# Last product of the down-projection rearranged, and the second block's mixer inputs begun earlier, in a one-core decoder layer

## Chip, cores and metric

The kernel runs on one core of one Trainium2 chip. The metric is the device time of one execution in microseconds (us). The kernel before takes 2018.15 us, the median of three runs (2018.1 to 2020.99).

## What is computed

One decoder layer on 2048 tokens of width 1024, all in float32. Cut to what matters here:

```python
h = rmsnorm(x, norm_mix) * (1 + sc_m) + sh_m          # mixer inputs
bg, cg, hc, u, v = split(h @ w_in)                    # 512 columns each
y_a = short_conv_mixer(bg, cg, hc, conv_w)            # gated convolution, 3 taps
y_b = chunked_sgu_mixer(gelu(u), gelu(v), v_norm, w_s, b_s)
x = x + g_m * (concat(rmsnorm(y_a), rmsnorm(y_b)) @ w_out)
h = rmsnorm(x, norm_ffn) * (1 + sc_f) + sh_f
gate, up = split(h @ w_up)                            # d_ff = 2816
x = x + g_f * ((silu(gate) * up) @ w_down)
return rmsnorm(x, norm_final)
```

A scaling, shift and gate for each channel (sc, sh, g) come from the conditioning vector.

## The kernel before

Tokens lie along the free dimension, channels on the partitions. The 2048 tokens are four quarters of 512 (`Q`), two quarters to a block (`NB = 2`). Each matrix product of two float32 tiles is made of three passes of TensorE over split operands (`mm3`, L173 to L175): the high half of both, high times low, low times high. The high half is made by a cast on ScalarE (L151), the low half by a subtraction on VectorE (L152), so a weight tile is ready only when both engines have handled it. L173 and L174 need the high half of the weights, L175 the low half.

The program does for each block: convolution and mixer (`mixer`: the products v, then u for each of the two quarters), the output projection (`out_proj`: 16 tiles, eight for each quarter, names w_o and o), and the preparation of the feed-forward inputs. Then come the up-projection and the down-projection of both blocks. `prepare(1, hT)` makes the second block's mixer inputs: for each of its two quarters eight loads of x (xin), eight squares on ScalarE with seven additions on GpSimd (sx), a sum over channels on TensorE (ms_x, L146), a reciprocal root (ScalarE and four VectorE steps), eight scalings on GpSimd (L262), eight shifts on ScalarE (L263) and eight splits (h). It is a generator: the output projection of the first block calls it three steps at a time after every tile.

Both feed-forward products are of Strassen's kind: seven products in place of eight. The last of the down-projection's seven, P2, multiplies left tiles A12 (one for each of 11 pairs of d_ff tiles, `NPR = 11`) with right tiles B21 that hold both blocks. For each pair and block it has 12 products (four output tiles, three passes). The second block follows three pairs behind the first (`lag = 3`). A left tile is split once, and both blocks use it. After P2 each block gets its last update of x (L787), the squares of the first quarter (L852), their sum (ms_f), the root, the final scaling (L870) and the stores to the output (L873). The second quarter (index i = 1) is ready before P2, and its final normalising is asked for during P2's first pair, for both blocks one after the other. In the last call three of the eight tiles go to ScalarE and GpSimd (L867, L868).

Each engine works its own list in order. The order in the lists comes from a scheduler that runs when the program is built. It moves instructions between the points where the program text has them, and names such as `tc.issue_after` bind some to others. Loads and stores all stand in SP's list. Tiles come from pools with a fixed number of buffers: 6 for split weights (`wslot`), 14 panels (inputs and right tiles), 17 temporaries, 8 PSUM banks.

Of the kernel before, what the change touches and what calls it, by code (L numbers as in the profile page):

```python
# [20 lines left out]
Q = 512  # L21
NQ = S // Q
NB = 2
# [4 lines left out]
NPR = NJ // 2  # L28
# [14 lines left out]
def trunk_kernel(  # L43
# [17 lines left out]
    nc = tc.nc  # L61
# [10 lines left out]
    def ps_tile(name):  # L72
        return psum.tile([P, Q], F32, tag="ps", name=name)
# [20 lines left out]
    ones_d = const.tile([P, P], F32, name="ones_d")  # L94
# [41 lines left out]
    def rms_finish(ms, n, name):  # L136
        r = tmp(f"R_{name}")[:, :n]
        rsqrt_into(r, ms, n)
        return r

    def rms_rows(sums, ones, name, ms=None):

        n = sums[0].shape[-1]
        ms = (ms or ps_tile(f"ms_{name}"))[:, :n]
        for k, s in enumerate(sums):
            nc.tensor.matmul(ms, ones, s, start=k == 0, stop=k == len(sums) - 1)  # L146
        return rms_finish(ms, n, name)
# [6 lines left out]
    last = {}  # L154
# [119 lines left out]
    class Conv:  # L274
# [30 lines left out]
        def normalise(self, i):  # L305
            r = rms_rows([self.acc[i]], ones_c, f"a{self.b}_{i}")
            for ct in range(CT):
                nc.vector.tensor_mul(self.ya[i][:, ct, :], self.ya[i][:, ct, :], r)
# [445 lines left out]
    def down(last_pair):  # L754
# [5 lines left out]
        def left(prod, p):  # L760
            w = wslot(f"{LEFT[prod]}_d{p}")
            name = LEFT[prod]
            if name[0] == "A":
                src = wts[U_FF + 3 * (2 * p + int(name[2]) - 1) + 2][:, 512 * (int(name[1]) - 1):][:, :512]
            else:
                src = sd[p][:, ("S2", "S1", "S4", "S3").index(name), :]
            raw = tmp(f"raw_{name}_d{p}")
            last["load"] = nc.sync.dma_start(raw, src).ins
            split(w, raw)
            return w  # L770

        def right(prod, p):
            t = panel(f"{RIGHT[prod]}_d{p}", [P, 2, NB * Q])
            raw = rawslot(f"raw_{RIGHT[prod]}_d{p}")
            nc.sync.dma_start(raw, gd[p][RIGHT[prod]].rearrange("p b q -> p (b q)"))
            split(t, raw)
            return [t[:, :, b * Q:b * Q + Q] for b in range(NB)]

        def products(prod, p, b, w, t, first):
            for s in range(4):  # L780
                ssl = slice(s * P, s * P + P)
                mm3(ps[b, s], w[:, 0, ssl], w[:, 1, ssl], t[:, 0, :], t[:, 1, :],
                    first and p == 0, p == NPR - 1, not first)

        def update(b, s, hi, i):
            dt = s + 4 * hi
            nc.vector.scalar_tensor_tensor(  # L787
                out=x[b][dt][:, i], in0=ps[b, s], scalar=gcol(dt), in1=x[b][dt][:, i], op0=ALU.mult, op1=ALU.add
            )
# [6 lines left out]
        for prod in ORDER_DOWN[:-1]:  # L796
# [17 lines left out]
            for b in range(NB):  # L814
                for s in range(4):
                    update(b, s, *lands[prod])
        lag = 3
        ready = {}
        for n in range(NPR + lag):
            while len(ready) < min(n + 4, NPR):  # L820
                ready[len(ready)] = left("P2", len(ready)), right("P2", len(ready))
            for b in range(NB):
                p = n - b * lag
                if p == 0:
                    for s in range(4):
                        ps[b, s] = ps_tile(f"d_P2_{b}_{s}")
                if 0 <= p < NPR:
                    w, t = ready[p]
                    products("P2", p, b, w, t[b], True)
            if n == 0:  # L830
                for f in fs:
                    f.squares(1, range(4))
                for f in fs:
                    f.normalise(1)
            for b in range(NB):
                if n == NPR - 1 + b * lag:
                    for s in range(4):
                        update(b, s, 0, 0)
                        fs[b].square(0, s)
            if n == NPR:  # L840
                fs[0].normalise(0)
        fs[1].normalise(0, (2, 5, 7))

    class Finish:

# [12 lines left out]
                square_into(acc, self.x[dt][:, i], dt == dts[0], nc.gpsimd)  # L858
            self.sums.setdefault(i, []).append(acc)

        def normalise(self, i, shared=()):

            r = rms_rows(self.sums[i], ones_d, f"f{self.b}_{i}")
            for dt in range(KT):
                xi = self.x[dt][:, i]
                if dt in shared:
                    nc.scalar.mul(xi, xi, vcol(V_NFIN + dt))  # L867
                    nc.gpsimd.tensor_mul(xi, xi, r)  # L868
                else:
                    nc.vector.scalar_tensor_tensor(  # L870
                        out=xi, in0=xi, scalar=vcol(V_NFIN + dt), in1=r, op0=ALU.mult, op1=ALU.mult
                    )
                nc.sync.dma_start(outT[QB * self.b + i, :, dt, :], xi)  # L873
# [127 lines left out]
    def stepper(g, n=1):  # L1001
        return lambda: [next(g, None) for _ in range(n)]

    hT, conv, ws_sb = start()
    y, late = mixer(0, hT, conv, ws_sb, lambda: None)
    hT = []
    g = prepare(1, hT)
    out_proj(0, y, late, stepper(g, 3))
    for _ in g:
        pass  # L1010
    g = ffn_inputs(0)
# [86 lines left out]
```

## Time and profile before

| | |
|---|---|
| median of three runs | 2018.15 us |
| the profiled execution | 2017.61 us |
| its span, first to last instruction | 2015.9 us |
| granted clock of TensorE, mean | 0.99 of 2.4 GHz |
| TensorE busy | 1951.1 us, 97% |
| VectorE busy | 1153.5 us, 57% |
| ScalarE busy | 786.8 us, 39% |
| GpSimd busy | 633.7 us, 31% |
| time in which DMA queue q1 had packets, of 16 engines | 47.3% |

TensorE is busy nearly throughout, so a profile of shares tells little. What can be saved is where TensorE waits, where its clock is at the lower level, and what lies behind its last product. Times in the views count from the start of the span. In the rows PE is TensorE, DVE is VectorE, ACT is ScalarE, POOL is GpSimd, SPq is the queue that issues DMAs.

### The profile page before, as it was taken

Reading aid. Unit: us, or ns where it says so; the run is one execution under the profiler, and the core shown is the slowest. Engines: PE = TensorE matmul, PEld = TensorE weight load, DVE = VectorE, ACT = ScalarE, POOL = GpSimd, SP = SyncE. Lnnn points to the kernel's source line nnn. Section 1 sums busy time; section 2 is a strip of 40 time slices with the busy share of each in tenths; the row PEclk is TensorE's granted clock in tenths of the full one; section 3 lists DMA queues with packets and bytes.
Section 4 is the critical chain, followed back from the end, with each engine's and each line's share of the span. In section 5 each row is a group of like instructions: output and inputs, shape, how many; then the busy total and the mean of one; then the engine's idle time right before and its main releaser. Section 6 shows DMA issues by size and latency. Waiting matters only on the chain.

```text
span 2015.9 us, 23007 instructions
## 1 busy us (share of the span) xinstructions
PE 1951.1 (97%) x8424; PEld 1583.6 (79%) x8424; DVE 1153.5 (57%) x1595; ACT 786.8 (39%) x1314; POOL 633.7 (31%) x440
## 2 busy tenths in 40 slices
PE   5989998999999999999999999999999999999996
PEld 3778876788878877878888888888888888888874
DVE  7988667543277574454455856455455454454464
ACT  3442655322366453333333633333333332233221
POOL 3200025100420145554644475665563100011011
PEclk9999999999999999999999999999999999999998
DMA  8567354231546635334324644543546974243332
GB/s 277 188 207 263 106 197 152 89 120 58 178 149 227 209 101 177 124 110 163 140 105 145 237 162 145 180 156 138 180 160 217 351 268 137 94 150 114 133 120 84
DMA packets 136915, 328.21 MB, mean 163 GB/s; under 512 B 14305, under 2 KB 22497, under 8 KB 134498
## 3 DMA queue, kind: packets, MB, share of 16 engines
q1 hardware_dynamic: 136802, 326.74, 47.3%
q8 instruction: 66, 1.08, 0.2%
q14 instruction: 47, 0.39, 0.1%
HBM read 242.28 MB, written 84.41 MB: 162 GB/s over the span
## 4 chain that ended last, share of the span: by engine, by line
PE 61%; DVE 4%; DMA 3%; POOL 1%; issue 1%; ACT 1%; SPq 0%; DVEq 0%; POOLq 0%; ACTq 0%
PE gu_a L173 7%; PE gu_a L174 7%; PE gu_a L175 7%; PE d_P L173 7%; PE d_P L174 7%; PE d_P L175 7%; PE gu_d L173 4%; PE gu_d L174 4%; PE gu_d L175 4%; PE gu_e L175 2%; PE gu_e L174 2%; PE gu_e L173 2%; DMA raw_gu<-in_wts 1%; DMA raw_T<-hd_T 1%; DVE x L870 0%
## 5 line engine op out<-in xcount | busy, mean ns | idle before, releaser
L152 DVE TENSOR_TENSOR ws<-raw_gu,ws 128x512 fp32r<-128x512 f32 x176 | 193.9, 1139 | 151.1 <-ACT ws L151 139.7
L152 DVE TENSOR_TENSOR A<-raw_gu,A 128x512 fp32r<-128x512 f32 x132 | 103.7, 818 | 127.1 <-ACT A L151 126.9
L151 ACT CAST ws<-raw_gu 128x512 fp32r<-128x512 f32 x176 | 101.9, 617 | 139.8 <-PE gu_d L175 67.7
L615 POOL TENSOR_TENSOR raw_gu<-raw_gu 128x512 f32<-128x512 f32 x44 | 59.5, 1353 | 289.6 <-DMA raw_gu<-in_wts 257.5
L173 PE MATMUL gu_a<-T,ws 128*128 128x512 f32 x352 | 139.4, 396 | 0.0
L174 PE MATMUL gu_a<-T,ws 128*128 128x512 f32 x352 | 139.0, 395 | 0.0
L175 PE MATMUL gu_a<-T,ws 128*128 128x512 f32 x352 | 138.9, 395 | 0.0
L133 POOL TENSOR_TENSOR sf<-sf,sq 128x512 f32<-128x512 f32 x18 | 28.3, 1576 | 327.5 <-ACT sq L132 326.5
L175 PE MATMUL c<-h,w_c 128*128 128x512 f32 x320 | 125.3, 392 | 4.8 <-DVE w_c L152 4.8
L173 PE MATMUL c<-h,w_c 128*128 128x512 f32 x320 | 125.6, 393 | 0.7 <-DVE ya L301 0.6
L174 PE MATMUL c<-h,w_c 128*128 128x512 f32 x320 | 125.1, 391 | 0.5 <-DVE h L224 0.5
L173 PE MATMUL d_P<-T_d,S_d 128*128 128x512 f32 x264 | 102.7, 389 | 0.0
L174 PE MATMUL d_P<-T_d,S_d 128*128 128x512 f32 x264 | 102.7, 389 | 0.0
L175 PE MATMUL d_P<-T_d,S_d 128*128 128x512 f32 x264 | 102.7, 389 | 0.0
L481 POOL TENSOR_TENSOR b<-b,r 128x512 f32<-128x512 f32 x32 | 43.5, 1379 | 185.8 <-DVE ya L301 87.8
L133 POOL TENSOR_TENSOR sx<-sx,sq 128x512 f32<-128x512 f32 x14 | 21.0, 1498 | 232.8 <-ACT sq L132 231.9
L151 ACT CAST A<-raw_gu 128x512 fp32r<-128x512 f32 x132 | 78.7, 620 | 39.5 <-DMA raw_gu<-in_wts 23.9
L152 DVE TENSOR_TENSOR S_d<-raw_S_d,S_d 128x512 fp32r<-128x512 f32 x44 | 32.1, 733 | 93.9 <-ACT S_d L151 93.7
L174 PEld LDWEIGHTS gu_a<-T,ws 128*128 128x128 f32 x352 | 66.0, 187 | 16.3 <-issue 0.2
L173 PEld LDWEIGHTS gu_a<-T,ws 128*128 128x128 f32 x352 | 66.0, 187 | 16.3 <-issue 0.2
L175 PEld LDWEIGHTS gu_a<-T,ws 128*128 128x128 f32 x352 | 66.0, 187 | 16.2
L624 POOL TENSOR_TENSOR raw_gu<-raw_gu 128x512 f32<-128x512 f32 x44 | 63.8, 1468 | 41.4 <-DVE A L152 41.4
(256 smaller groups left out, 5528.5 us busy)
## 6 DMA issues: line engine op xcount, KB each, us to landing
raw_gu<-in_wts SPq DMA_DIRECT2D x88, 512.0 KB, 4.1
raw_T_d<-gd_T SPq DMA_DIRECT2D x44, 512.0 KB, 3.7
raw_B_d<-gd_B SPq DMA_DIRECT2D x33, 512.0 KB, 3.5
wm<-in_wmodT SPq DMA_DIRECT2D x32, 512.0 KB, 4.3
raw_o<-in_wts SPq DMA_DIRECT2D x32, 512.0 KB, 5.7
raw_c<-in_wts SPq DMA_DIRECT2D x28, 512.0 KB, 4.1
gd_B<-s SPq DMA_DIRECT2D x44, 256.0 KB, 7.0
gd_T<-s SPq DMA_DIRECT2D x44, 256.0 KB, 2.1
```

What stands on the lines that cost most here:

```text
L133: (add or nc.vector).tensor_add(acc, acc, sq)
L151: nc.scalar.copy(dst[:, 0, :], src)
L152: (sub or nc.vector).tensor_sub(dst[:, 1, :], src, dst[:, 0, :].bitcast(F32))
L173: nc.tensor.matmul(ps, l_hi, r_hi, start=start, stop=False, skip_group_check=onto)
L174: nc.tensor.matmul(ps, l_hi, r_lo, start=False, stop=False, skip_group_check=onto)
L175: nc.tensor.matmul(ps, l_lo, r_hi, start=False, stop=stop, skip_group_check=onto)
L481: nc.gpsimd.tensor_mul(t, t, rs[i])
L615: nc.gpsimd.tensor_add(a21, a21, a22)
L624: nc.gpsimd.tensor_sub(a12, a12, a11)
```

## The change

There are two parts.

In the program's end (`down`), the second block follows six pairs behind the first. Left tiles are loaded and split for each block by itself, three pairs ahead; right tiles three pairs ahead. The normalising of the second quarter stands after the third pair for the first block and after the fifth for the second block. The first block's last normalising (ScalarE multiplies, GpSimd scales, all eight tiles) stands after pair 6 of the second block. The second block's last three pairs are done output tile by output tile: nine products, then one sum matmul for the tile before (ms_last), the update and the square. The last scaling is all on VectorE.

In the mixer, `prepare` is called from the mixer of the first block after 14 steps without work, one step at a time, and in the output projection two steps at a time in place of three.

```diff
-        def products(prod, p, b, w, t, first):
-            for s in range(4):
+        def products(prod, p, b, w, t, first, ss=range(4)):
+            for s in ss:
...
-        lag = 3
-        ready = {}
+        lag = 6
+        rights, lefts = {}, {}
         for n in range(NPR + lag):
-            while len(ready) < min(n + 4, NPR):
-                ready[len(ready)] = left("P2", len(ready)), right("P2", len(ready))
+            while len(rights) < min(n + 3, NPR):
+                rights[len(rights)] = right("P2", len(rights))
             for b in range(NB):
                 p = n - b * lag
+                for k in range(5 if n == NPR + 1 else 3):
+                    if 0 <= p + k < NPR and (b, p + k) not in lefts:
+                        lefts[b, p + k] = left("P2", p + k)
...
-                if 0 <= p < NPR:
-                    w, t = ready[p]
-                    products("P2", p, b, w, t[b], True)
+                if 0 <= p < NPR - 3 * b:
+                    products("P2", p, b, lefts[b, p], rights[p][b], True)
             if n == 0:
                 for f in fs:
                     f.squares(1, range(4))
-                for f in fs:
-                    f.normalise(1)
...
-            if n == NPR:
-                fs[0].normalise(0)
-        fs[1].normalise(0, (2, 5, 7))
+            if n in (2, 4):
+                fs[n // 2 - 1].normalise(1)
+            if n == NPR - 1:
+                for s in range(4):
+                    update(0, s, 0, 0)
+                    fs[0].square(0, s)
+            if n == NPR + 1:
+                fs[0].normalise(0, spare=True)
+        for s in range(4):
+            for p in range(NPR - 3, NPR):
+                products("P2", p, 1, lefts[1, p], rights[p][1], True, [s])
+            if s == 0:
+                ms = ps_tile("ms_last")
+            nc.tensor.matmul(ms, ones_d, fs[1].sums[0][s], start=s == 0, stop=False)
+            update(1, s, 0, 0)
+            fs[1].square(0, s)
+        nc.tensor.matmul(ms, ones_d, fs[1].sums[0][4], start=False, stop=True)
+        fs[1].normalise(0, rms_finish(ms, Q, "last"))
...
-    y, late = mixer(0, hT, conv, ws_sb, lambda: None)
-    hT = []
-    g = prepare(1, hT)
-    out_proj(0, y, late, stepper(g, 3))
+    h0, hT = hT, []
+    def later():
+        for _ in range(14):
+            yield
+        yield from prepare(1, hT)
+    g = later()
+    y, late = mixer(0, h0, conv, ws_sb, stepper(g))
+    out_proj(0, y, late, stepper(g, 2))
```

How the lists of the engines stand. First SP, where the loads of the second block's first quarter (xin) are issued; raw_o are the weights of the output projection, x_0 the first block's residual, xd its copy in memory. Before:

```order
L158 DMA raw_o_0_1_2234<-in_wts 128x1024
L422 DMA x_0_1_2165<-in_xT 128x2x512 x2
L158 DMA raw_o_0_2_2311<-in_wts 128x1024
L158 DMA raw_o_0_3_2358<-in_wts 128x1024
L158 DMA raw_o_0_4_2415<-in_wts 128x1024
L158 DMA raw_o_0_5_2467<-in_wts 128x1024
L422 DMA x_0_2_2166<-in_xT 128x2x512 x2
L422 DMA x_0_3_2167<-in_xT 128x2x512 x2
L434 DMA xd_0_168<-x_0_0_2164 128x512
L232 DMA xin_0_2213<-in_xT 128x512
```

and changed:

```order
L158 DMA raw_o_0_1_2271<-in_wts 128x1024
L232 DMA xin_0_1878<-in_xT 128x512
L232 DMA xin_1_1880<-in_xT 128x512
L232 DMA xin_2_1882<-in_xT 128x512
L232 DMA xin_3_1884<-in_xT 128x512
L232 DMA xin_4_1886<-in_xT 128x512
L232 DMA xin_5_1888<-in_xT 128x512
L232 DMA xin_6_1890<-in_xT 128x512
L232 DMA xin_7_1892<-in_xT 128x512
L422 DMA x_0_1_2204<-in_xT 128x2x512 x2
```

The eight loads stand before the output projection's third weight tile, where they stood behind the first store of its result.

Second, VectorE in P2, around the normalising of the second quarter: R_f0_1 and R_f1_1 are the roots of blocks 0 and 1, x2 the tiles that are scaled, A12_d the left tiles by pair. Before:

```order
L124 SCALAR_TENSOR_TENSOR R_f0_1_14160<-a_14163,R_f0_1_14160 128x512
L120 SCALAR_TENSOR_TENSOR y_14189<-ms_f1_1_14184,y_14189 128x512
L870 SCALAR_TENSOR_TENSOR x2_0_0_11821<-x2_0_0_11821,vec_180,R_f0_1_14160 128x512 x2
L870 SCALAR_TENSOR_TENSOR x2_0_1_11893<-x2_0_1_11893,vec_180,R_f0_1_14160 128x512 x2
L870 SCALAR_TENSOR_TENSOR x2_0_2_11965<-x2_0_2_11965,vec_180,R_f0_1_14160 128x512 x2
L870 SCALAR_TENSOR_TENSOR x2_0_3_12037<-x2_0_3_12037,vec_180,R_f0_1_14160 128x512 x2
L121 SCALAR_TENSOR_TENSOR a_14190<-y_14189 128x512
L124 SCALAR_TENSOR_TENSOR R_f1_1_14187<-a_14190,R_f1_1_14187 128x512
```

and changed:

```order
L124 SCALAR_TENSOR_TENSOR R_f0_1_14194<-a_14197,R_f0_1_14194 128x512
L881 SCALAR_TENSOR_TENSOR x2_0_0_11821<-x2_0_0_11821,vec_180,R_f0_1_14194 128x512 x2
L881 SCALAR_TENSOR_TENSOR x2_0_1_11893<-x2_0_1_11893,vec_180,R_f0_1_14194 128x512 x2
L881 SCALAR_TENSOR_TENSOR x2_0_2_11965<-x2_0_2_11965,vec_180,R_f0_1_14194 128x512 x2
L881 SCALAR_TENSOR_TENSOR x2_0_3_12037<-x2_0_3_12037,vec_180,R_f0_1_14194 128x512 x2
L152 TENSOR_TENSOR A12_d5_14223<-raw_A12_d5_14224,A12_d5_14223 128x512
L152 TENSOR_TENSOR A12_d6_14245<-raw_A12_d6_14246,A12_d6_14245 128x512
L152 TENSOR_TENSOR A12_d0_14262<-raw_A12_d0_14263,A12_d0_14262 128x512
L119 TENSOR_TENSOR y_14272<-R_f1_1_14270 128x512
```

Three splits of left tiles stand between the two normalisings now; after the second normalising the next split is that of A12_d7.

Third, the end of TensorE's list; sf and sq are squares, ms_f1_0 and ms_last their sum, d_P2_1_3 the last output tile of the second block. Before:

```order
L173 MATMUL d_P2_1_3_14280<-B21_d10_14400,A12_d10_14395 128x512
L174 MATMUL d_P2_1_3_14280<-B21_d10_14400,A12_d10_14395 128x512
L175 MATMUL d_P2_1_3_14280<-B21_d10_14400,A12_d10_14395 128x512
L146 MATMUL ms_f1_0_14591<-sf_1_0_13554,ones_d_181 128x512
L146 MATMUL ms_f1_0_14591<-sq_14580,ones_d_181 128x512
L146 MATMUL ms_f1_0_14591<-sq_14583,ones_d_181 128x512
L146 MATMUL ms_f1_0_14591<-sq_14586,ones_d_181 128x512
L146 MATMUL ms_f1_0_14591<-sq_14589,ones_d_181 128x512
```

and changed:

```order
L848 MATMUL ms_last_14615<-sq_14631,ones_d_181 128x512
L173 MATMUL d_P2_1_3_14351<-B21_d8_14321,A12_d8_14529 128x512
L174 MATMUL d_P2_1_3_14351<-B21_d8_14321,A12_d8_14529 128x512
L175 MATMUL d_P2_1_3_14351<-B21_d8_14321,A12_d8_14529 128x512
L173 MATMUL d_P2_1_3_14351<-B21_d9_14364,A12_d9_14534 128x512
L174 MATMUL d_P2_1_3_14351<-B21_d9_14364,A12_d9_14534 128x512
L175 MATMUL d_P2_1_3_14351<-B21_d9_14364,A12_d9_14534 128x512
L173 MATMUL d_P2_1_3_14351<-B21_d10_14403,A12_d10_14539 128x512
L174 MATMUL d_P2_1_3_14351<-B21_d10_14403,A12_d10_14539 128x512
L175 MATMUL d_P2_1_3_14351<-B21_d10_14403,A12_d10_14539 128x512
L848 MATMUL ms_last_14615<-sq_14644,ones_d_181 128x512
L851 MATMUL ms_last_14615<-sq_14657,ones_d_181 128x512
```

Two of the five sum matmuls stand behind the last product, where all five did; the other three stand between the output tiles.

## Rows read from the trace of the kernel before

**Rows 1.** Waits of TensorE: line, releaser, us in total, times, longest

```profile
PE ms_x L146 <- POOL sx L133: 8.4, 2, 5.4
...
PE o L173 <- ACT w_o L151: 3.6, 2, 2.0
...
PE ms_f L146 <- POOL sf L133: 2.1, 1, 2.1
```

**Rows 2.** Timeline, TensorE, first output projection: start, us, instruction, [idle before <-releaser]

```profile
297.14 2.07 PE L146 MATMUL ms_x<-sx,ones_d 128*128 128x512 f32 x2 [2.98 <-POOL sx L133]
...
299.86 0.51 PE L175 MATMUL o<-ya,w_o 128*128 128x512 f32 x1
...
340.48 2.08 PE L146 MATMUL ms_x<-sx,ones_d 128*128 128x512 f32 x2 [5.42 <-POOL sx L133]
...
344.48 0.40 PE L175 MATMUL o<-ya,w_o 128*128 128x512 f32 x1
```

**Rows 3.** The chain that ended last, TensorE in P2: start, us, instruction

```profile
1979.61 0.23 PE d_P L174
...
1981.43 4.30 PE ms_f L146 x10
```

**Rows 4.** Stretches: length, busy time by engine, granted clock, DMA share, GB/s

```profile
303.00:321.00 18.00, 16.03 (x71) 13.00 (x70) 14.83 (x14) 12.22 (x21) 12.32 (x8) 1.00 0.08 30
...
338.00:347.00 9.00, 6.52 (x18) 4.56 (x19) 5.76 (x8) 1.94 (x3) 2.88 (x3) 0.64 0.54 179
```

**Rows 5.** Timeline, other engines, first mixer and output projection; xin's time to landing

```profile
285.62 11.46 POOL L133 TENSOR_TENSOR sx<-sx,sq 128x512 f32<-128x512 f32 x7 [217.22 <-ACT sq L132]
302.99 12.33 POOL L262 TENSOR_TENSOR xin<-xin,R_x 128x512 f32<-128x512 f32 x8 [5.90 <-DVE R_x L124]
...
303.13 1.70 DVE L152 TENSOR_TENSOR w_o<-raw_o,w_o 128x512 fp32r<-128x512 f32 x1 [0.22 <-ACT w_o L151]
...
320.88 0.68 DVE L152 TENSOR_TENSOR w_o<-raw_o,w_o 128x512 fp32r<-128x512 f32 x1
...
250.90 1.67 DVE L369 TENSOR_SCALAR u<-u,rt_y 128x512 f32<-128x512 f32 x4
...
260.52 2.42 ACT L318 ACTIVATE yb<-tr,vec 128x512 fp32r<-128x512 f32 x4
...
DMA to landing us min/median/max: 3.7/6.5/7.0
```

**Rows 6.** Timeline, P2: TensorE, ScalarE, VectorE and the DMA queue

```profile
1926.98 1.12 PE L146 MATMUL ms_f<-sf,ones_d 128*128 128x512 f32 x2 [2.10 <-POOL sf L133]
...
1931.82 0.39 PE L174 MATMUL d_P<-B_d,A_d 128*128 128x512 f32 x1
...
1924.11 1.28 ACT L116 ACT_TABLE_LOAD   x1 [2.39 <-PE ms_f L146]
...
1930.74 5.38 DVE L870 SCALAR_TENSOR_TENSOR x<-x,vec,R_f 128x512 f32<-128x512 f32 x8
...
1938.26 5.18 SPq L873 DMA_DIRECT2D outT<-x  x8
1943.53 3.19 SPq L768 DMA_DIRECT2D raw_A_d<-in_wts  x6
...
1946.88 0.62 ACT L151 CAST A_d<-raw_A_d 128x512 fp32r<-128x512 f32 x1 [4.66 <-DMA raw_A_d<-in_wts]
```

**Rows 7.** Timeline and chain behind the last product

```profile
1990.83 0.40 PE L175 MATMUL d_P<-B_d,A_d 128*128 128x512 f32 x1
...
1995.23 2.06 DVE L787 SCALAR_TENSOR_TENSOR x<-d_P,mod,x 128x512 f32<-128x512 f32 x3
...
1996.01 0.64 ACT sq L852
...
1996.69 4.45 PE ms_f L146 x6
...
2004.86 6.42 DVE L870 SCALAR_TENSOR_TENSOR x<-x,vec,R_f 128x512 f32<-128x512 f32 x5
```

More of the change, by code (lines that the diff above doesn't have):

```diff
@@ L832, in down @@
                     f.squares(1, range(4))
-                for f in fs:
-                    f.normalise(1)
[L835 to L839, printed above, removed]
-            if n == NPR:
-                fs[0].normalise(0)
-        fs[1].normalise(0, (2, 5, 7))
+            if n in (2, 4):
[16 more added lines that the diff above has]
+        fs[1].normalise(0, rms_finish(ms, Q, "last"))
     class Finish:
@@ L859, in squares, with normalise @@
             self.sums.setdefault(i, []).append(acc)
-        def normalise(self, i, shared=()):
-            r = rms_rows(self.sums[i], ones_d, f"f{self.b}_{i}")
+        def normalise(self, i, r=None, spare=False):
+            if r is None:
+                r = rms_rows(self.sums[i], ones_d, f"f{self.b}_{i}")
             for dt in range(KT):
                 xi = self.x[dt][:, i]
-                if dt in shared:
+                if spare:
                     nc.scalar.mul(xi, xi, vcol(V_NFIN + dt))
```

## The prediction

> **What bounds the kernel.** The page's busy shares come first: TensorE is busy for 97% of the span, so an edit to another engine counts only where TensorE waits for it, or behind TensorE's last product. The second view is the list of TensorE's waits [rows 1]. Of its entries three touch the change: two waits of 8.4 us in all for GpSimd's additions of squares (ms_x), 3.6 us for weights of the output projection, and 2.1 us for GpSimd's additions before the final normalising (ms_f). The reader is to see that both ms_x waits end on sx, the very work that the change begins earlier.
>
> Third is TensorE's timeline at these places [rows 2]. A wait costs more than its length. In the chain one product follows the last after 0.23 us, and ten sum matmuls take 4.30 us, so the two records of one sum take 0.86 [rows 3]. After the first ms_x wait of 2.98 us the sum starts at 297.14 and the third product behind it at 299.86; at the pace just named it would be at about 298.3. So 1.6 us are lost to a lower clock. After the second wait (5.42 us) the sixth product is at 344.48 and would be at 342.3: 2.2 us lost. The granted clock of that stretch is 0.64, that is a mixture of the two levels 2.4 and 1.2 GHz; in a stretch that holds a 2.0 us wait for weights it stays at 1.00 [rows 1, 4]. A wait of two us for weights costs just itself, then, and these longer ones cost half as much again.
>
> Fourth is what lies behind the last product [rows 7]. That product ends at 1991.2; the span ends at 2015.9. These 24.7 us hold nothing of TensorE but five sums.
>
> **The change part by part: the mixer inputs.** The eight loads of the first quarter's x move in SP's list from behind the first stored result of the output projection to behind its second weight load. Their squares and additions then run in the mixer. GpSimd's seven additions take 11.46 us [rows 5]; moved ahead by over 30 us they end long before the sum is wanted. The first ms_x wait goes with its clock loss: 2.98 + 1.6 = 4.6 us. The second quarter's loads move ahead of the fourth weight load of the second half, about two tiles of 24 products (2 x 5.5 us), while the place of its sum stays; the wait was 5.42. It goes too: 5.42 + 2.2 = 7.6 us.
>
> What is this bought with? ScalarE gets eight squares and GpSimd eleven us of additions in the mixer. Beside GpSimd a split of 128x512 takes VectorE 1.70 us, alone 0.68 [rows 5]. The work there that TensorE waits for next is the scaling of u, at 250.9 to 252.6, whose transposed result ScalarE takes only at 260.5 [rows 5]: doubled, it still has over 6 us. The loads pass raw_o_0_2 and the residual's loads in SP's list, none of which TensorE needs within 20 us. xin took up to 7.0 us to land, and ScalarE would wait at the first square for a late one. I put all of this at nothing; uncovered it is what the third rival costs.
>
> One wait stays and moves. GpSimd's eight scalings of xin (12.33 us) and the splits of h stand ahead of a weight split, before the eighth tile's second half and now before the sixth tile. The walk is the same, but in the change four evictions of the transposes (2.42 us on ScalarE) stand among them. I take 0.3 us more than before; the bounds are 2 us less (the wait goes) and 3 us more. Sum of this part: -4.6 - 7.6 + 0.3 = **-11.9 us**.
>
> **The end, inside P2.** The wait of 2.10 us goes, since the sum now stands behind three pairs (36 products, 8.3 us) instead of one. With it goes the slow stretch: the tenth product after the first is at 1931.82 and would be at about 1929.9 [rows 6], so 1.9 us. That is -4.0.
>
> Three of the last five sums move from behind the last product to before it: 3 x 0.86 = +2.6.
>
> Eleven left tiles are loaded and split a second time. The casts and subtractions (0.62 [rows 6] and 0.68 [rows 5] us each) fit in VectorE's idle time on average; the order is what matters. Take the end of the first sum as M. ScalarE loads its table (1.28 us [rows 6]), the root and VectorE's four steps take 3.72 (from the end of the sums at 2001.14 to the first scaling at 2004.86 [rows 7]), eight scalings 5.38 [rows 6], and only then comes the split of A12_d5 (0.68): M + 11.1. TensorE meanwhile has pairs 3 and 4 (24 products, 5.5 us), the other sum (1.7 for two), and 14 products that need no low half (3.2): M + 10.4. A wait of about 0.7. Then three splits, the second root and eight scalings: A12_d7's low half comes at M + 21.4, while TensorE has work to about M + 19.8. A wait of about 1.6. After that left tiles come from memory behind sixteen stores to the output: the store issue ended at 1943.4, and the load issued then was cast at 1946.88, 3.4 us later [rows 6]; one step of two blocks is 5.5 us, so this keeps up. Together +2.3; bounds 0 (the scheduler's fill suffices) and 9 (both waits longer by a landing of 3.4).
>
> **Behind the last product.** Now [rows 7]: three updates wait until 1995.23 for eight scalings of the other block, the squares follow, the sums run at the lower clock (4.45 us), then root and four steps to 2004.86, five scalings beside GpSimd in 6.42, and 4.6 to the end. Changed: one update 0.75; its square 0.68; the last sum 0.90; root and steps 3.72; eight scalings alone 5.38; the last store and the end 4.6. Sum 16.0. So 24.7 - 16.0 = -8.6.
>
> Here a cover is needed. The first block's eight scalings on GpSimd, 1.54 each [rows 5], start about 8.0 us after its sum begins (4.3 for the sum, 3.7 for the root) and end at 20.3. The last product ends at 4.3 + 2.8 + 8.3 + 2.6 = 18.0. GpSimd thus ends 2.3 us behind the last product, and VectorE's root begins at 3.1. If GpSimd is late, the root's steps and the scalings are stretched as the split was, by at most 1.8 us in the four steps and the first two scalings.
>
> The Trainium skill, "SBUF — State Buffer", section "Who interferes with whom", says that a VectorE instruction with two inputs in SBUF contends with a GpSimd instruction that reads SBUF. The rows agree (0.68 against 1.70 us). By that rule alone, with GpSimd itself held up in the tail, the sum would be 1.8 us smaller.
>
> Sum of this part: -4.0 + 2.6 + 2.3 - 8.6 = **-7.7 us**. Both parts: -19.6 us from 2017.6 of the profiled execution gives 1998.0. That execution lies 0.5 under the median of the runs, so I say **1998.5 us**.
>
> **Rivals.**
>
> The end's gain is eaten (14%). VectorE's two normalisings hold left tiles back longer than the walk says, 9 us and more in place of 2.3, and the clock falls in it as after ms_x. For it: VectorE's list has eight scalings in one piece ahead of the splits. Against it: before, TensorE came through sixteen scalings in one piece with no listed wait for A_d. Then this part gives about zero and the time is 2017.6 + 0.5 - 11.9 = 2006.
>
> The mixer's gain is eaten (10%). The sums are ready, but TensorE waits at the same place for weights, because splits take 1.70 us beside GpSimd, and ScalarE stands at a late xin. For it: in the first half of the output projection the h block stands two tiles earlier, before six weight casts. Against it: three tiles of weights are split ahead. The time is 2018.1 - 7.7 = 2010.5. If both are eaten (6%), nothing is left: 2018.
>
> The slower side (4%): starvation. If, when a normalising starts, no left tile in split form is left, each costs TensorE table (1.3), root and steps (3.7), scalings (5.4), a landing (3.4) and cast and split (1.3): 15 us, twice, so 30 in place of 2.3, and the time is 1998.5 + 27.7 = 2026. It decides from waits of 22 us in P2 on.
>
> **How the numbers follow.** The forecast has 66%. Its own range takes the bounds: 2 us less in the mixer and 2.3 in P2 below, 3, 6.7 and 1.8 above, not all at once: 1994 to 2007. That reaches the first rival; with the second rival and the rest left out, the range for 8 in 10 is 1994 to 2007.5. A change under 0.2% (4 us) can't be told from none with this kernel. Faster is the forecast, the first two rivals and a part of what is left over: 0.89. Same 0.06, slower 0.05.
>
> **What would show it.** In the changed profile: no wait of ms_x for sx, and a granted clock near 1.00 in the output projection; a wait for w_o of about two us at the sixth tile; no wait of ms_f for sf; two short waits of d_P for A_d after pairs 4 and 6; from the last product to the end 16 us, with updates that wait for TensorE alone, and eight scalings in 5.4 us. Waits for A_d of over 9 us, or w_o waits of over 8, would make the prediction wrong.

## The result and the profile after

The changed kernel takes 2002.32 us (median of four runs, 1998.67 to 2004.81) against 2018.12 us of the kernel before beside it (2016.58 to 2020.99). The ratio is 0.9919, 95% interval 0.9900 to 0.9938: 15.8 us less. The forecast was 1998.5 with a range of 1994.0 to 2007.5.

The profiled execution of the changed kernel is the longest of its four: 2004.81 us, span 2003.0. Its list of TensorE's waits (line, releaser; us in total, times, longest), as [rows 1]:

```profile
PE o L173 <- ACT w_o L151: 4.5, 2, 3.0
PE u L174 <- DVE w_u L152: 3.2, 1, 3.2
PE gu_a L173 <- DVE c L667: 2.7, 2, 2.1
...
PE d_P L175 <- DVE A_d L152: 1.8, 2, 1.0
...
PE ms_last L851 <- ACT sq L862: 0.6, 1, 0.6
...
PE d_P L173 <- ACT A_d L151: 0.3, 1, 0.3
```

The two waits of ms_x for GpSimd's sx and the one of ms_f for sf are gone. New are three short waits of d_P for A_d, 2.1 us in all. The wait for w_o has grown from 3.6 to 4.5. The waits of u and gu_a, which the change does not touch, are longer by 1.1 and 1.0.

Second, the timeline behind the last product (start, us, engine, instruction, [idle before <-releaser]), as [rows 7]:

```profile
1978.32 10.00 POOL L879 TENSOR_TENSOR x<-x,R_f 128x512 f32<-128x512 f32 x8 [56.00 <-DVE R_f L124]
...
1987.72 0.39 PE L175 MATMUL d_P<-B_d,A_d 128*128 128x512 f32 x1
1987.96 1.02 PE L848 MATMUL ms_last<-sq,ones_d 128*128 128x512 f32 x2
1988.16 0.75 DVE L787 SCALAR_TENSOR_TENSOR x<-d_P,mod,x 128x512 f32<-128x512 f32 x1 [2.19 <-PE d_P L175]
...
1989.62 1.12 PE L851 MATMUL ms_last<-sq,ones_d 128*128 128x512 f32 x2 [0.65 <-ACT sq L862]
...
1991.51 0.69 DVE L119 TENSOR_TENSOR y<-R_last 128x512 f32<-128x512 f32 x1 [2.60 <-ACT R_last L116]
...
1993.68 0.69 DVE L124 SCALAR_TENSOR_TENSOR R_last<-a,R_last 128x512 f32<-128x512 f32 x1
1994.41 5.39 DVE L881 SCALAR_TENSOR_TENSOR x<-x,vec,R_last 128x512 f32<-128x512 f32 x8
```

The last product ends at 1988.1 and the span 14.9 us later, in place of 24.7. One update, one square, the sum, the root and eight scalings stand in a row, as forecast. GpSimd's eight scalings take 1.25 us each and end at 1988.32, just behind the last product.

Third, P2 around the two normalisings, as [rows 6] (SPq: the queue that issues DMAs):

```profile
1929.59 5.39 DVE L881 SCALAR_TENSOR_TENSOR x<-x,vec,R_f 128x512 f32<-128x512 f32 x8
...
1930.37 4.97 SPq L884 DMA_DIRECT2D outT<-x  x8
...
1934.90 1.89 DVE L152 TENSOR_TENSOR A_d<-raw_A_d,A_d 128x512 fp32r<-128x512 f32 x3
1935.43 1.44 SPq L768 DMA_DIRECT2D raw_A_d<-in_wts  x3
1935.64 1.20 PE L175 MATMUL d_P<-B_d,A_d 128*128 128x512 f32 x4 [0.75 <-DVE A_d L152]
```

The split of A12 comes only behind VectorE's eight scalings, and the product that needs its low half waits 0.75 us. The forecast had 0.7 there.

Where did the time go, stage by stage? For this the span is divided at five matmuls: A from the first product of the first output projection to the sum over channels behind it; B to the first product of the up-projection; C to the first of the down-projection; D to the last product (the whole down-projection, with P2 as its last part); E from that product's start to the end of the span. All of it is read from TensorE's timeline, in us, for every kernel that ran with a profile here; the times were rounded to 0.1 first, so the last digit can be off by one:

| kernel | A | B | C | D | E | D+E |
|---|---|---|---|---|---|---|
| before | 140.7 | 291.7 | 857.7 | 430.4 | 25.1 | 455.5 |
| changed, first profile | 130.6 | 293.2 | 860.3 | 432.3 | 15.3 | 447.6 |
| r_after | 130.6 | 290.1 | 860.0 | 432.2 | 15.3 | 447.5 |
| r_mixer_only | 130.6 | 290.1 | 859.4 | 428.8 | 26.7 | 455.5 |
| r_end_only | 140.3 | 290.8 | 859.8 | 432.0 | 15.3 | 447.3 |
| r_pairwise_end | 132.3 | 289.9 | 859.5 | 429.2 | 16.9 | 446.1 |
| r_start10 | 125.7 | 293.0 | 860.2 | 431.7 | 15.3 | 447.0 |
| r_norm_early | 131.8 | 292.1 | 859.0 | 444.0 | 15.3 | 459.3 |
| r_end_vector | 132.0 | 292.4 | 858.0 | 432.0 | 15.3 | 447.3 |
| r_lag3_spare | 138.7 | 292.7 | 859.3 | 428.9 | 18.5 | 447.4 |
| r_lag3_mix | 132.5 | 291.4 | 860.9 | 430.4 | 18.6 | 449.0 |
| r_lag3_mix_01 | 132.1 | 289.9 | 857.9 | 427.6 | 18.6 | 446.2 |
| r_lag3_mix_12 | 131.7 | 292.8 | 858.8 | 426.9 | 18.5 | 445.4 |
| r_pairwise_spread | 132.0 | 292.0 | 860.3 | 428.7 | 17.0 | 445.7 |

A and D+E carry the change. B and C, which no edit aims at, move by over three us from profile to profile, also where the order is the same (B of the changed kernel is 293.2 and 290.1).

### The profile page after: what moved, and what is told of

Same layout as the page of the kernel before. It is cut to its first block, busy times and chain, and to the rows that moved or that the text cites. A ratio compares the mean times of both kernels' runs of the same rounds, so it can differ in the third digit from the quotient of the medians.

```text
span 2003.0 us, 23081 instructions
## 1 busy us (share of the span) xinstructions
PE 1949.3 (97%) x8424; PEld 1582.6 (79%) x8424; DVE 1148.4 (57%) x1601; ACT 794.9 (40%) x1330; POOL 638.9 (32%) x445
## 4 chain that ended last, share of the span: by engine, by line
PE 60%; DVE 4%; DMA 4%; POOL 1%; issue 1%; ACT 1%; SPq 1%; DVEq 0%; POOLq 0%; ACTq 0%
PE gu_a L173 7%; PE gu_a L174 7%; PE gu_a L175 7%; PE d_P L173 7%; PE d_P L175 7%; PE d_P L174 7%; PE gu_d L174 4%; PE gu_d L173 4%; PE gu_d L175 4%; PE gu_e L175 2%; PE gu_e L174 2%; PE gu_e L173 2%; DMA raw_gu<-in_wts 2%; DMA b<-xd 1%; DVE x L881 1%
## 5 line engine op out<-in xcount | busy, mean ns | idle before, releaser
L152 DVE TENSOR_TENSOR ws<-raw_gu,ws 128x512 fp32r<-128x512 f32 x176 | 189.8, 1115 | 150.3 <-ACT ws L151 149.8
L615 POOL TENSOR_TENSOR raw_gu<-raw_gu 128x512 f32<-128x512 f32 x44 | 59.1, 1344 | 291.2 <-DMA raw_gu<-in_wts 255.5
L151 ACT CAST S_d<-raw_S_d 128x512 fp32r<-128x512 f32 x44 | 27.3, 621 | 132.2 <-PE d_P L175 118.4
L175 PEld LDWEIGHTS gu_a<-T,ws 128*128 128x128 f32 x352 | 66.0, 187 | 16.1
```

The source lines that it names most:

```text
L151: nc.scalar.copy(dst[:, 0, :], src)
L152: (sub or nc.vector).tensor_sub(dst[:, 1, :], src, dst[:, 0, :].bitcast(F32))
L175: nc.tensor.matmul(ps, l_lo, r_hi, start=False, stop=stop, skip_group_check=onto)
L615: nc.gpsimd.tensor_add(a21, a21, a22)
```

## The experiments

Each ran in five rounds beside the kernel before. That kernel's median was 2017.29 us for the first four (r_after to r_pairwise_end), 2018.48 for the next four and 2017.79 for the last four.

**r_after: the changed kernel again.** No edit.

> The changed kernel once more, as it is. Theory A (the losses of the profiled execution outside the change, 2.6 us at the up-projection's inputs, 1.5 us at the second mixer's u and 1.0 us at the start, differ from execution to execution): median 1999 to 2004 us, and in this profile the waits of gu_a for c and of u for w_u are back at about 1.7 and 2.1 us, or elsewhere, so that the span differs by some us from that of the first profile. Theory B (the change brings them): the same waits of 2.7 and 3.2 us stand there again and the mixer's gain at the first down-projection product is again 5.0 us and not 7.6. In both, 14 to 16 us lie behind the last product, and no ms_x or ms_f wait for GpSimd is listed.

Measured: 2001.18 us, ratio 0.9917 (0.9904 to 0.9929); profiled span 1999.5. The wait of u is back at 2.0 and that of gu_a at 0.7; B is 3.1 us shorter than in the first profile. So those losses differ between executions (theory A). A, D and E repeat within 0.1 us.

**r_mixer_only.** The kernel before, with this alone:

```diff
-    y, late = mixer(0, hT, conv, ws_sb, lambda: None)
...
-    out_proj(0, y, late, stepper(g, 3))
+    y, late = mixer(0, h0, conv, ws_sb, stepper(g))
+    out_proj(0, y, late, stepper(g, 2))
```

> The kernel before with the mixer part alone. Forecast's theory: both ms_x waits and their slow clock go, 11.9 us less by the sum, 10.1 us less by the first profile of the changed kernel, so a ratio to the kernel before of 0.9940 to 0.9950, about 2006 to 2008 us. Rival (a part is given back in the second mixer and the up-projection because all that follows meets another rhythm): 5 us less, ratio 0.9975, with longer waits of u and gu_a than before. Behind the last product still 24 to 25 us.

Measured: 2008.82 us, ratio 0.9964 (0.9952 to 0.9976), 8.5 us less. That lies between the forecast's theory (0.9940 to 0.9950) and the rival (0.9975); the interval leaves out the first and just holds the second, and by the ratio the gain is 7.3 us. So the time alone does not decide. A is 130.6 in this profile, 10.1 less than before, and the mixer ahead of it keeps its length (52.5 us from the first product of u to A, as before). The rival has time given back in B and C, with longer waits of u and gu_a. Here u waits 2.1 and gu_a 1.4 (before 2.1 and 1.7), and B and C together are 1149.5 against 1149.4. As such sums differ by up to six us between profiles, the average says more: 1150.7 over the three kernels with the old order of the mixer, 1150.8 over the ten with the new one. Nothing is given back; the gain is smaller than forecast because A is mostly longer than in this profile (below).

One expectation failed: behind the last product stand 26.3 us in place of 24 to 25. Three of the sums there ran longer than the 4.45 us of before [rows 7] (timeline, TensorE):

```profile
1986.32 5.49 PE L146 MATMUL ms_f<-sq,ones_d 128*128 128x512 f32 x6 [3.79 <-ACT sq L852]
```

The rest is a longer way from the last scaling to the end of the span, 5.2 us for 4.6. D is 1.6 shorter in the same profile, by the clock (below), and makes up for it.

**r_end_only.** The kernel before, with `down` and `Finish` of the changed one.

> The kernel before with the end part alone. Forecast's theory: 7.7 us less by the sum; by the first profile of the changed kernel P2 costs 1.9 us and the stretch behind the last product gains 9.8, together 7.9 us less, ratio 0.9961, about 2010 us. If the parts don't touch one another, this ratio and that of the mixer part multiply to that of the changed kernel. Rival (the two parts share a gain or disturb one another): the two differ from the whole by over 3 us. Both ms_x waits are still listed, u and gu_a wait as in the kernel before.

Measured: 2009.63 us, ratio 0.9961 (0.9949 to 0.9973), 7.7 us less, as expected. D costs 1.6 and E gains 9.8. The waits of u (2.9) and gu_a (2.4) are long in this kernel too, which has no mixer part: they do not come from it. The two ratios multiply to 0.9925, the whole has 0.9917 (0.9904 to 0.9929): within the intervals the parts add up.

**r_pairwise_end.** The changed kernel with

```diff
-                if 0 <= p < NPR - 3 * b:
+                if 0 <= p < NPR:
...
-            for p in range(NPR - 3, NPR):
-                products("P2", p, 1, lefts[1, p], rights[p][1], True, [s])
...
+        fs[1].normalise(0)
```

> The changed kernel with the second block's last three pairs done pair by pair as all others, then the four updates, the squares and all five sums; the first block stays six pairs ahead and the last scaling on VectorE. Theory A (the gain behind the last product comes from the lag of six, by which the updates no longer stand behind eight scalings of the other block): five sums of 0.86 us start at the last product and end about 4.5 us behind it in place of 2.8, while three sums of 0.86 us less stand before it: -1 to +1 us against the changed kernel. Theory B (it comes from the tile-by-tile order): the sums run at the lower clock behind the last product, 4.5 us for three of them as in the kernel before, and the updates stand in a row: 2 to 4 us longer than the changed kernel, with 18 to 20 us behind the last product.

Measured: 1999.55 us, ratio 0.9911 (0.9898 to 0.9924); the changed kernel beside it had 2001.18. By the medians that is 1.6 less, by the ratios 1.2, a little beyond theory A's -1 to +1 and not clear of noise. D is 3.0 shorter, E 1.6 longer. Its end on TensorE (timeline):

```profile
1980.28 0.40 PE L175 MATMUL d_P<-B_d,A_d 128*128 128x512 f32 x1
1980.52 1.02 PE L146 MATMUL ms_f<-sf,ones_d 128*128 128x512 f32 x2
1981.37 3.60 PE L146 MATMUL ms_f<-sq,ones_d 128*128 128x512 f32 x8
```

All five sums run behind one another with no wait: by the time TensorE reaches a square's sum, the square is there. So the tile-by-tile order gains nothing (theory A). The three sums that it takes from behind the last product stand ahead of it instead.

**r_start10.** `for _ in range(14)` becomes `range(10)`.

> The changed kernel with the second block's mixer inputs begun after 10 idle steps in place of 14, so that the first sum stands inside the mixer and the walk of scalings, shifts and splits two tiles earlier in both halves of the output projection. Theory A (what the mixer part lost of its forecast is the w_o wait at the end of each walk, 1.5 and 3.0 us, the second with a granted clock of 0.91 over 20 us): earlier walks leave the weight splits time, the waits shrink, and the output projection's 130.6 us become 127 to 130; 1 to 4 us less than the changed kernel. Theory B (the walk is paced by GpSimd's 1.5 us a tile and the wait only moves with it): the waits stay at 4.5 us in all, or the mixer's own products wait as well: 0 to 4 us more.

Measured: 2001.8 us, ratio 0.9917 (0.9904 to 0.9930), no difference. The waits for w_o shrink to 1.2 and A to 125.7, further than theory A's 127 to 130. But the mixer ahead grows from 52.5 to 57.7 us, where two new waits stand (timeline, TensorE):

```profile
258.28 1.12 PE L146 MATMUL ms_x<-sx,ones_d 128*128 128x512 f32 x2 [1.21 <-POOL sx L133]
271.95 3.72 PE L359 MATMUL mx<-v,cw 128*128 128x256 f32 x16 [2.59 <-DVE yb L319]
```

Both together are 183.4 us against 183.1: the wait is only moved, as theory B had it.

**r_norm_early.** The changed kernel with both normalisings of the second quarter back in the step n == 0:

```diff
-            if n in (2, 4):
-                fs[n // 2 - 1].normalise(1)
...
+                for f in fs:
+                    f.normalise(1)
```

> The changed kernel with the second quarter's final normalising asked for during the first pair of P2 for both blocks at once, as before. Theory A (the forecast's term of 4.0 us: a wait of 2.1 and a stretch at the lower clock): the wait of ms_f for GpSimd's sf is listed again with about 2 us and the span from the first product of P2 to the last grows by 2 to 4 us. Theory B (the waits for A12's low halves, 1.8 us in all, come from the later scalings and go when these stand early): the two cancel, 0 to 1 us of difference. A wait for A_d of over 5 us would say that the early scalings hold back the left tiles more than the late ones.

Measured: 2013.96 us, ratio 0.9978 (0.9970 to 0.9987), some 12 us more than the changed kernel by the ratios. That is beyond both theories; the third case named, a wait for A_d of over 5 us, came. The wait of ms_f is there again (2.1), and with it (waits, then the DMA queue's timeline):

```profile
PE d_P L173 <- ACT A_d L151: 8.8, 2, 7.1
```

```profile
1923.79 4.97 SPq L884 DMA_DIRECT2D outT<-x  x8
1928.85 0.41 SPq L768 DMA_DIRECT2D raw_A_d<-in_wts  x1
1930.54 4.97 SPq L884 DMA_DIRECT2D outT<-x  x8
1935.60 11.55 SPq L768 DMA_DIRECT2D raw_A_d<-in_wts  x18
```

The stores stand in the queue ahead of the loads of A12 and wait for VectorE's scalings. One load gets through at 1928.85; the next 18 follow only at 1935.60. ScalarE, which casts these tiles, stands still until a load lands (timeline):

```profile
1932.26 0.62 ACT L151 CAST A_d<-raw_A_d 128x512 fp32r<-128x512 f32 x1 [11.16 <-DMA raw_A_d<-in_wts]
```

TensorE waits 7.1 and 1.7 us, its granted clock is 0.78 over the 15 us from 1920 and 0.88 over the next 15, and D grows by 11.8. This is the starvation that the prediction priced, at 30 us, as its slower rival. In the changed kernel, with the normalisings later, its waits for A_d stay at 2.1 in all. The early place alone does not bring it: r_mixer_only and r_lag3_spare have it too, with the lag of three and shared left tiles, and list no wait for A_d.

**r_end_vector.** `fs[0].normalise(0, spare=True)` becomes `fs[0].normalise(0)`.

> The changed kernel with the first block's last normalising on VectorE in place of ScalarE and GpSimd. Theory A (the tail is short because the updates of the second block find VectorE free): eight scalings of 0.67 us start where GpSimd's did, about 9.4 us ahead of the last product, and end 4 us ahead; the first tile's update and square then come about 3 us after the sum that needs them, TensorE waits 3 us once, with or without a fall of the clock: 3 to 5 us more than the changed kernel. Theory B (VectorE has room there, since it idles 2.2 us between updates): no wait, within 1 us of the changed kernel. Behind the last product 15.3 us in both.

Measured: 2001.61 us, ratio 0.9918 (0.9904 to 0.9932), no difference; D 432.0, E 15.3 (timeline):

```profile
1974.74 5.39 DVE L881 SCALAR_TENSOR_TENSOR x<-x,vec,R_f 128x512 f32<-128x512 f32 x8
1980.05 2.06 DVE L787 SCALAR_TENSOR_TENSOR x<-d_P,mod,x 128x512 f32<-128x512 f32 x3
...
1981.51 1.98 PE L848 MATMUL ms_last<-sq,ones_d 128*128 128x512 f32 x4
```

The updates do stand behind the eight scalings, until 1980.05. But the scheduler put two of the sums together at 1981.51, where their squares are ready, so nothing waits (theory B). With the lag of six the first block's scalings need not leave VectorE.

**r_lag3_spare.** The kernel before, with the exchange of engines alone:

```diff
-                fs[0].normalise(0)
-        fs[1].normalise(0, (2, 5, 7))
+                fs[0].normalise(0, range(8))
+        fs[1].normalise(0)
```

> The kernel before with the lag of three, the shared left tiles and the early normalising kept; only the first block's last normalising goes to ScalarE and GpSimd for all eight tiles, and the very last one to VectorE for all eight. Theory A (what counts is that the scalings of the other block leave VectorE, whatever the lag): the updates no longer wait for eight scalings, and 17 to 19 us lie behind the last product in place of 25, P2 as before: 6 to 8 us less than the kernel before, ratio 0.9960 to 0.9970. Theory B (the lag of six is needed): GpSimd's scalings start only about at the last product and run for 10 to 12 us beside VectorE's updates, root steps and scalings, which then take up to 1.7 us each in place of 0.7: 22 us or more behind the last product, under 3 us gained, ratio over 0.9985.

Measured: 2011.46 us, ratio 0.9961 (0.9947 to 0.9975), 7.0 us less. D+E is 447.4 in this profile, 447.3 in r_end_only: this two-line edit gives what the whole end part gives (theory A), though 1.6 of it are a clock that here stayed at 1.00 in P2 (below). Its end (timeline):

```profile
1989.10 2.75 DVE L787 SCALAR_TENSOR_TENSOR x<-d_P,mod,x 128x512 f32<-128x512 f32 x4
1989.35 10.77 POOL L868 TENSOR_TENSOR x<-x,R_f 128x512 f32<-128x512 f32 x8 [60.98 <-DVE R_f L124]
...
1990.66 0.40 PE L175 MATMUL d_P<-B_d,A_d 128*128 128x512 f32 x1
1991.75 3.60 PE L146 MATMUL ms_f<-sq,ones_d 128*128 128x512 f32 x8
...
1996.18 1.15 DVE L119 TENSOR_TENSOR y<-R_f 128x512 f32<-128x512 f32 x1 [4.33 <-ACT R_f L116]
1997.36 0.69 DVE L120 SCALAR_TENSOR_TENSOR y<-ms_f,y 128x512 f32<-128x512 f32 x1
1998.08 0.91 DVE L121 SCALAR_TENSOR_TENSOR a<-y 128x512 f32<-128x512 f32 x1
1999.03 1.63 DVE L124 SCALAR_TENSOR_TENSOR R_f<-a,R_f 128x512 f32<-128x512 f32 x1
2000.70 5.39 DVE L870 SCALAR_TENSOR_TENSOR x<-x,vec,R_f 128x512 f32<-128x512 f32 x8
```

The updates no longer wait for scalings of the other block, and end while the sums run. From the end of the last product to the end of the sums pass 4.3 us where 9.9 passed before [rows 7], 5.6 less. The last scalings, all on VectorE, take 5.39 for 6.42, and the way from there to the end 3.1 for 4.6, another 2.5 less. Against it stands GpSimd, which works until 2000.12: three of the four root steps beside it are stretched, 4.4 us in place of 2.8. That is the 1.6 us by which E is longer than in r_pairwise_end. The two halves of the exchange were not run apart.

**r_lag3_mix.** The same edit with the mixer part.

> The kernel before with the mixer part of the change and, of the end part, only the exchange of engines (first block's last normalising on ScalarE and GpSimd, the very last on VectorE); lag of three, shared left tiles, early normalising. Theory A (the lag, the left tiles loaded twice and the tile-by-tile end gain nothing of their own): the output projection takes 130.6 us, 18.5 us lie behind the last product's start, and the time is that of the changed kernel within 2 us, 1999 to 2003, ratio 0.9905 to 0.9925. Theory B (the end part's other edits are needed once the mixer part is in): 3 us or more above the changed kernel.

Measured: 2005.44 us, ratio 0.9935 (0.9920 to 0.9949), 3.6 us above the changed kernel by the ratios, though the intervals overlap. It misses theory A's range (1999 to 2003) and by its number fits theory B's 3 us or more. By the stages, A is 1.9 above the shortest and D 1.5 above r_lag3_spare, both by the clock (below); C is the longest of all. So what the stages show is the clock and the spread of C, and no new wait in P2. Whether the rest is a loss of its own stays open; the next two kernels, which keep the lag of three and the shared left tiles, do without it.

**r_lag3_mix_01 and r_lag3_mix_12.** The last kernel, with the second quarter's normalising one pair later: in the first of the two only for the second block, in the other, which has (1, 2) for (0, 1), for both:

```diff
-                for f in fs:
-                    f.normalise(1)
+            for f, m in zip(fs, (0, 1)):
+                if n == m:
+                    f.normalise(1)
```

> The kernel of r_lag3_mix with the second block's early normalising asked for one pair later, the first block's left where it was. Theory A (the wait of 2.1 us of ms_f for GpSimd's sf, and 1.9 us of slow clock behind it, are the second block's alone): both go and no wait for A_d comes, 3 to 4 us less than r_lag3_mix. Theory B (the later scalings hold up left tiles, as in the kernel with a lag of six): a wait for A_d of 1 to 9 us takes their place, 0 to 8 us more.

> The kernel of r_lag3_mix with the early normalising after the second pair for the first block and after the third for the second block. Theory A: as for the kernel with 0 and 1, the wait and the slow clock go, 3 to 4 us less than r_lag3_mix. Theory B: the two pieces of eight scalings now stand nearer to the last left tiles split ahead, waits for A_d of 1 to 9 us, 0 to 8 us more; if only this one of the two shows it, the distance to the splits decides.

Measured: 1999.45 us, ratio 0.9913 (0.9898 to 0.9928), and 2000.11, ratio 0.9911 (0.9897 to 0.9925). That is 6.0 and 5.3 less than r_lag3_mix by the medians, 4.4 and 4.8 by the ratios, where 3 to 4 were expected. The wait of ms_f is gone in both, and with it the low clock behind it; D falls by 2.8 and 3.5. No wait for A_d appears; the first has one of 0.7 for the root (waits):

```profile
PE d_P L173 <- DVE y L120: 0.7, 1, 0.7
```

Theory A holds for both in mechanism; what the times differ beyond D is within the spread of B and C. These two have the lag of three, load each left tile once, and take the same time as the changed kernel.

**r_pairwise_spread.** r_pairwise_end with the scalings as a generator, two after each pair step:

```diff
-                fs[n // 2 - 1].normalise(1)
+                spread.append(fs[n // 2 - 1].pieces(1))
+            for g in spread:
+                next(g, None)
+                next(g, None)
```

> The kernel of r_pairwise_end (lag of six, last pairs done pair by pair) with the second quarter's eight scalings for each block asked for two at a time after each pair step in place of all at once. Theory A (the two waits for A12's low halves, 1.8 us in all, are VectorE's eight scalings in one piece): they go, 2 to 3 us less than r_pairwise_end, 1997 to 1998. Theory B (they come from the root's four steps, or from the stores ahead of the loads in the DMA list): they stay, within 1 us.

Measured: 1998.91 us, ratio 0.9908 (0.9893 to 0.9923). The two waits are replaced by one of 1.65 us (timeline):

```profile
1937.18 0.88 SPq L768 DMA_DIRECT2D raw_A_d<-in_wts  x2
1938.15 4.30 SPq L876 DMA_DIRECT2D outT<-x  x5
...
1941.11 1.14 ACT L151 CAST A_d<-raw_A_d 128x512 fp32r<-128x512 f32 x2
1941.78 0.50 PE L173 MATMUL d_P<-B_d,A_d 128*128 128x512 f32 x1 [1.65 <-ACT A_d L151]
```

The load issued at 1937.18, behind seven stores, is cast at 1941.11, so D is only 0.5 shorter: theory B, the stores ahead of the loads. It is the lowest median of all, but no version here is measurably faster than the changed kernel.

## Why the prediction held, and which terms were mis-sized

**The mixer's waits: right.** Both waits of ms_x are gone, the mixer keeps its 52.5 us, and the work moved into it costs nothing.

**The moved wait for w_o: mis-sized.** The forecast added 0.3 us, and nothing for the clock, with the step "a wait of two us for weights costs just itself", which it had from one row. The waits went from 1.97 and 1.62 to 1.46 and 2.99, together 0.9 more. And the clock fell, to a mixture of 2.4 and 1.2 GHz (stretches as [rows 4]: length, busy time by engine, granted clock, DMA share, GB/s; first r_after, then r_pairwise_end):

```profile
301.00:311.00 10.00, 8.30 (x36) 6.25 (x35) 8.78 (x14) 6.31 (x12) 0.00 (x0) 1.00 0.60 178
340.00:358.00 18.00, 15.01 (x60) 11.79 (x59) 16.34 (x18) 13.30 (x24) 10.01 (x7) 0.91 0.16 51
```

```profile
300.00:310.00 10.00, 8.61 (x30) 6.62 (x30) 7.97 (x14) 5.57 (x11) 0.00 (x0) 0.83 0.67 211
```

0.91 over 18 us is 1.6 us lost after the wait of 2.99. In the second kernel a wait of 1.49 us, at the same place as one of 1.46 in the first, costs 1.7 more (0.83 over 10 us). So -12.2 + 0.9 + 1.6 = -9.7, against -10.1 measured in three profiles. The other seven kernels that share this order show 131.7 to 132.5, on average 132.1, each with more time at the low clock (0.86 over the 12 us from 300, or 0.83 in place of 0.91 over the 20 us from 340). Over all ten A is 131.6. The three kernels with the old order average 139.9. The gain is thus 8.3 us, near what r_mixer_only measured (8.5 by the medians, 7.3 by the ratio), in place of 11.9. Of the 3.6 us between, 0.8 is that the forecast started from a profile whose A (140.7) is above that average; the rest is the longer waits and the clock behind them.

**P2: right on the waits, too much for the clock, too little for the sums.** Waits for A_d of 0.7 and 1.6 were forecast; 0.75, 1.0 and 0.3 came, 2.1 in place of 2.3, and 1.8 in r_after and r_end_only. For the wait of ms_f the forecast took 2.1 and a slow stretch of 1.9. Two kernels with the same wait show that the second half does not always come (timeline and stretch of r_mixer_only, then of r_lag3_mix):

```profile
1918.21 1.12 PE L146 MATMUL ms_f<-sf,ones_d 128*128 128x512 f32 x2 [2.10 <-POOL sf L133]
```

```profile
1918.00:1930.00 12.00, 11.79 (x50) 9.45 (x51) 11.79 (x18) 0.69 (x1) 0.15 (x1) 1.00 0.53 188
```

```profile
1921.26 1.97 PE L146 MATMUL ms_f<-sf,ones_d 128*128 128x512 f32 x2 [2.09 <-POOL sf L133]
```

```profile
1918.00:1930.00 12.00, 9.91 (x32) 6.61 (x31) 9.37 (x14) 2.66 (x3) 3.12 (x2) 0.86 0.21 80
```

After 2.10 us the clock stays at 1.00 and D is 428.8; after 2.09 us it is 0.86 and D is 430.4. The four kernels with the old P2 have 428.8, 428.9, 430.4 and 430.4. The changed kernel's 432.2 costs 1.8 to 3.4 where 0.9 was forecast. The other term is the work itself: without its waits and at a clock of 1.00, D is 428.8 - 2.1 = 426.7 in r_mixer_only and 432.0 - 1.8 = 430.2 in r_end_only, 3.5 more, where 2.6 was forecast for the three sums that move. In r_pairwise_end, where they don't move, it is 429.2 - 1.8 = 427.4; so 2.8 come with the tile-by-tile order and 0.7 with the rest of the end part.

**Behind the last product: right, a little better.** 9.8 us gained in the profile, 8.6 forecast. The last store and the end took 3.2 us (1999.80 to 2003.0) in place of 4.6. It is 3.1 to 3.2 in all twelve profiles in which VectorE does all the last scalings, and 4.6 and 5.2 in the two in which GpSimd has three of them. The cover held, with more room than the forecast's 0.8 us, since GpSimd's scalings took 1.25 us and not 1.54: the root steps took 0.69 each. What happens when it does not hold is r_lag3_spare: three steps with all inputs in SBUF (the memory of the kernel's tiles) are stretched, while the one that reads ms_f from PSUM, where TensorE's results land (L120), keeps its 0.69. The Trainium skill, "SBUF — State Buffer", section "Who interferes with whom", says that a VectorE instruction with two inputs in SBUF contends with a GpSimd instruction that reads SBUF. The trace agrees: of these four steps the three of that kind took 1.15, 0.91 and 1.63 us.

**The reason given for that gain** was right: the updates no longer stand behind scalings. But the prediction did not see how little it takes: with the lag of three it is enough that the scalings leave VectorE (r_lag3_spare), and with the lag of six they need not even do that (r_end_vector; the lag alone was not run). On top of the exchange the lag of six, the second loading of the left tiles and the tile-by-tile end add nothing that a later normalising does not (r_lag3_mix_01 and _12); against r_lag3_spare r_end_only loses 3.1 us in D and gains 3.2 in E.

**The sum.** The parts alone give 8.5 + 7.7 = 16.2 us, the whole 15.8 and 16.1 in its two measurements; forecast 19.6. What is missing is 3.6 by the averages of A, most of it the w_o term with its clock. P2's extra cost (0.9 to 2.5) and the better tail (1.2) about cancel, which the forecast can take no credit for. The rivals that left only one part's gain did not come; the starving one needs the old place of the normalising with the changed kernel's left tiles (r_norm_early).

## What to carry to other kernels

When one part of a change could have come alone, test it alone: exchanging two engines' scalings gave 7.0 us in two lines, about as much as a rearranged product that loads its left tiles twice (7.7). A wait that is moved must be priced where it lands, with the waits it makes behind it: four steps earlier it went from the output projection into the mixer, unchanged in sum. And stores that waited for arithmetic held up the loads behind them in SP's list until TensorE stood for 7.1 us (r_norm_early), so the place of a store in the list can count more than its own time.

## What the runs showed of the hardware

The granted clock after a short wait is not the same in every execution. After waits of 1.46 and 1.49 us at one place it was 1.00 and 0.83, after 2.10 and 2.09 us at another 1.00 and 0.86. At the first place all ten kernels with the new mixer order waited 1.45 to 1.49 us: over the 12 us from 300 the clock was 0.86 in three of them and 1.00 in seven. So the 1.6 to 1.7 us behind such a wait come or don't, and what decides it was not found.

The up-projection (C) took 857.9 to 860.9 us in ten profiles of kernels with the same mixer order, and the stage before it 289.9 to 293.2. Some of it stands in the waits of u and gu_a, which differ between two executions of the same kernel (3.2 and 2.7 us, then 2.0 and 0.7). What sets them was not found. A single pair of profiles of these kernels can't tell a difference of three us.
